# Two attention stages taken out of the scheduler's hands: every engine issues in emission order there

## The chip, the cores and the metric

The kernel runs on one core of a Trainium2 chip. The metric is the device time of one execution in microseconds. Before the change the median of 3 runs is 2639.24 us (2636.28 to 2641.58). The engines are named as in the profile: PE (TensorE matmul), PEld (its weight load), DVE (VectorE), ACT (ScalarE), POOL (GpSimd), SP (SyncE, which issues the DMAs).

## The reference

Two layers of a streaming encoder on 1024 tokens of width 1024, batch 1. Cut to what matters:

```python
for layer in range(DEPTH):                       # DEPTH = 2
    h = modulate(rms_norm(x, ln_mix_g[layer]), sh1, sc1)
    if layer % 2 == 0:
        mix = even_mixer(...)   # q,k,v,u = split(h @ w_in); concat[A, B] @ w_out
    else:
        mix = odd_mixer(...)    # cq..cg, dq,dk,dv = split(h @ w_in); concat[C, D] @ w_out
    x = x + g1[:, None, :] * mix
    x = x + g2[:, None, :] * swiglu(modulate(rms_norm(x, ...), sh2, sc2), w_in, w_out)

# A: 8 heads of 64, softmax over the own and 8 previous chunks of 64 frames, with a position bias
# B: state space model, complex diagonal scan over time, then gelu and a sigmoid gate (GLU)
# C: retention, 4 heads of 128:
scores = jnp.einsum('bhid,bhjd->bhij', qn, kn) * intra_decay
out = (jnp.einsum('bhij,bhjd->bhid', scores, vn)
       + jnp.einsum('bhid,bhde->bhie', qn * q_decay[:, :, None], state))
state = state * chunk_decay[:, None, None] + jnp.einsum('bhjd,bhje->bhde', kn * k_decay[:, :, None], vn)
# ... then (o - mu) * rsqrt(var + EPS) * norm_g, times silu(gate)
# D: stick-breaking attention, 8 heads of 64, blocks of 128 queries
log_1m_beta = jnp.where(causal, -jax.nn.softplus(z), 0.0)
between = lax.cumsum(log_1m_beta, axis=3, reverse=True) - log_1m_beta
w = jnp.where(causal, jnp.exp(jax.nn.log_sigmoid(z) + between), 0.0)
```

## The kernel before, in words

The program emits its instructions from Python generators. A generator yields where its next part has to wait, with the number of ticks to wait; `pipe.tick` advances all of them by one tick. The Tile framework then orders what was emitted: it knows which instruction needs which, and its scheduler chooses, on each engine, in which order they are issued. Only the order within an engine can change. What an instruction needs from another engine is a semaphore wait, and the PSUM banks and the numbered buffers of a pool (`bufs=`) are given out in turn, so that an instruction may also wait for the last reader of its buffer.

The first stage, AB, is `ab_phase` (61 steps). Each step starts one attention unit, `a_unit`: one head and 128 queries. It computes up to two groups of scores (L498, tile `mm` in three banks), adds the bias and takes the maximum on DVE (L597, L600), the exponential on ACT (L605), transposes on PE (L510), copies them out on ACT (L512, tile `pts`), and weighs the values on PE (L521). After four units of both heads of a pair, half a head pair is finished: a reciprocal (L617), a broadcast on POOL (L619), transposes (L626), then L630 on ACT, L631 on DVE, L632 on ACT and L633 on DVE, each needing the one before. Every five steps `s5_block` handles a block of the state space model: loads (tiles `u`, `m`, `e`), matmuls (L964), on DVE six operations (L970 to L972, twice), four scans (L976) and a complex product (L698 to L703, helper `cmul`), then matmuls again (L985, L987). Near the end, `glu` follows.

The second stage, CD, is `cd_phase`: 32 steps n of four ticks. Each step has one `c_tile` (retention, one head and 128 tokens) and one `d_unit` (stick-breaking, one head, the query blocks i and 7 - i). In `c_tile` PE projects 128 tokens in four parts of six 512-column matmuls (L248 to L250, tile `mm`); DVE makes L1078 and L1079 of it, ACT the copies L1080 and L1082, POOL the sum L1084; PE transposes that (L1089), ACT copies it (L1091), DVE scales it (L1092, L1094); PE makes the scores and the new state (L1097, L1099), DVE masks them (L1101, L1108), PE multiplies with values and state (L1112, L1114) into a bank `ob`; DVE takes mean and variance of it (L1117, L1118), POOL the power (L1119, L1120), and DVE normalises (L1122, tile `co`). Every fourth step `c_tail` adds a gate (L1132 on ACT, L1133 on POOL, L1135 on DVE, L1139 on PE, L1146 on ACT).

In `d_unit` PE makes three groups of scores (L498, tile `at`, four banks for all of CD), DVE adds the mask to two of them (L1185), ACT takes two sigmoids of each (L1188, tile `w`, and L1189, tile `b`), DVE runs two product scans over `w` (L1197; together 1152 columns), and L1199 multiplies them into `b`. Three ticks later PE transposes `b` (L510), ACT copies it (L512), and in every second step PE weighs the values (L521). Between the ticks a weight stream (`pump`) loads the next projection weights: a cast on ACT (L141) and a subtraction on POOL (L142).

Of the kernel before, what the change touches and what calls it, by code (L numbers as in the profile page):

```python
# [1368 lines left out]
def build(ctx, tc, I, out):  # L1369
    k = Trunk(ctx, tc, I, out)  # L1370
    nc, pipe = tc.nc, k.pipe
    k.cond()


    with tc.tile_pool(name="pp", bufs=1, reuse_waits="tile") as pp:
        with tc.tile_pool(name="first", bufs=1, reuse_waits="tile") as xp:
            k.first(pp, xp)
        with tc.tile_pool(name="heads", bufs=1, reuse_waits="tile") as hp:
            with tc.tile_pool(name="qk", bufs=1, reuse_waits="tile") as qp:
                right = ExitStack()  # L1380
                sp = right.enter_context(tc.tile_pool(name="set0", bufs=1, side="right", reuse_waits="tile"))
                k.stream.low = nc.vector
                for n, _ in enumerate(k.a_dense(qp)):
                    if n == 2:
                        setup = k.s5_setup(sp)
                        pipe.start(setup)
                    if n in (19, 32):
                        pipe.start(k.ada(qp, 0, 2 if n == 19 else 4))
                    if n == 38:
                        k.a_open(hp)  # L1390
                    if n == 46:
                        assert setup.gi_frame is None
                        right.close()
                        ap = right.enter_context(tc.tile_pool(name="mixa", bufs=1, side="right", reuse_waits="tile"))
                        k.pp = pp
                    pipe.tick(*([k.a_step(hp, ap, n - 46)] if n >= 46 else []))
                k.stream.low = nc.gpsimd
                pipe.tick(k.a_step(hp, ap, 2))
            k.ab_phase(hp, ap, 3)
            right.close()  # L1400
            k.pp = None
    with tc.tile_pool(name="xp0", bufs=1, reuse_waits="tile") as xp:
        x = [xp.tile([P, T], F32, name=f"x{n}") for n in range(NK)]
        for n in range(NK):
            nc.sync.dma_start(out=x[n], in_=I["x"][n])
        pipe.start(k.ada(xp, 0, 3))
        k.out_proj(xp, 0, x, [0, 1, 2, 4, 5, 6, 7, 3], 5, [(0, 4), (0, 3)], [k.ada(xp, 0, 5)])

        def done(n, h):
            if h:  # L1410
                nc.sync.dma_start(out=k.xd[n], in_=x[n])
            k.stat(xp, x[n], n, h)
            if n == NK - 1:
                pipe.start(k.norm(xp, x, h, [(1, 1), (1, 0)]))

        k.ffn(xp, 0, x, done, [lambda l=l, p=p: k.ada(xp, l, p) for l, p in ((1, 1), (1, 0), (1, 2), (1, 4), (1, 3))])
        for t in range(4):
            pipe.tick(k.v_tile(xp, "hf", k.wdv, t))
            pipe.tick()
        pipe.drain()  # L1420


    with tc.tile_pool(name="dense1", bufs=1, reuse_waits="tile") as dp:
        for n, _ in enumerate(k.d_dense(dp)):
            pipe.tick()
            if n == 1:
                for t in range(4, NT):
                    pipe.tick(k.v_tile(dp, "ve", k.wdv, t))
                    pipe.tick()
                k.wdv.free()  # L1430
    right = ExitStack()
    cp = right.enter_context(tc.tile_pool(name="mixc", bufs=1, side="right", reuse_waits="tile"))
    with tc.tile_pool(name="mixd", bufs=1, reuse_waits="tile") as dp:
        k.c_setup(cp)
        k.cd_phase(dp, cp)
    with tc.tile_pool(name="xp1", bufs=1, reuse_waits="tile") as xp:
        x = [xp.tile([P, T], F32, name=f"x{n}") for n in range(NK)]
        for kk in (0, 1, 2, 4, 5, 6):
            pipe.tick(k.mix_split(kk))
        pipe.tick(k.mix_split(3, 512))  # L1440
        for n in range(NK):
            nc.sync.dma_start(out=x[n], in_=k.xd[n])
        pipe.tick()
        while k.tail.gi_frame is not None:
            pipe.tick()
        right.close()
        k.out_proj(xp, 1, x, [0, 1, 2, 4, 5, 6, 7, 3], 1, [(1, 4), (1, 3)], [k.ada(xp, 1, 5)])

        def done(n, h):
            nc.sync.dma_start(out=out[n, :, h * 512:h * 512 + 512], in_=x[n][:, h * 512:h * 512 + 512])  # L1450

        k.ffn(xp, 1, x, done)
# [93 lines left out]
```

## Time and profile before

| | us |
|---|---|
| median of 3 runs (range) | 2639.24 (2636.28 to 2641.58) |
| the profiled execution | 2628.13 |
| its span | 2626.3 |
| busy in the span: PE, DVE, POOL, ACT | 2535.4, 1134.9, 809.5, 708.9 |
| stage AB (262 to 475 us of the span): PE, DVE, ACT, POOL busy of 213 | 190.25, 107.00, 145.29, 44.52 |
| stage CD (1448 to 1805 us): PE, DVE, ACT, POOL busy of 357 | 340.44, 242.03, 172.55, 127.79 |

The span is the profiled execution without what lies around it (1.8 us here). Busy time adds the drawn lengths of an engine's instructions, overlaps counted once. The mean granted clock of PE in the span is 0.992 of full speed. The rest of the span is dense projections and feed-forward layers, where PE is busy nearly all the time.

### The profile page before, as it was taken

The page shows a single profiled execution, that of the slowest core. Times are in us where ns is not written, and L with a number is a line of the kernel's source. Part 1 is how long each engine was busy: PE and PEld are TensorE (multiplying, and loading weights), DVE is VectorE, ACT ScalarE, POOL GpSimd, SP SyncE. Part 2 cuts the span into 40 slices and gives each one's busy share as a digit, 9 for nine tenths or more (in the row PEclk, how much of TensorE's full clock was granted, in tenths as well). Part 3 has the DMA queues.
Part 4 walks back from the last instruction along what each step waited for, and adds up shares of the span by engine and source line. Part 5 has one row for each costly group of instructions (what it writes and reads, how often), then busy time and mean ns, then how long its engine had stood idle before and what let it go on. Part 6 is the DMA issues. An engine that isn't in the chain of part 4 may idle for free. (4 is left out here: it accounts for less than half of the span.)

```text
span 2626.3 us, 32531 instructions
## 1 busy us (share of the span) xinstructions
PE 2535.4 (97%) x12912; PEld 2104.9 (80%) x12912; DVE 1134.9 (43%) x2058; ACT 708.9 (27%) x1293; POOL 809.5 (31%) x538
## 2 busy tenths in 40 slices
PE   6999898999999999999999999999999999999999
PEld 4898776777888888888788778887788888888887
DVE  6576563474333322222531566765632222222223
ACT  4332568322111111111232444544231111111100
POOL 3465003423222222232212143423243333333311
PEclk9999999999999999999999999999999999999999
DMA  7287764543233311111234333224311111111101
GB/s 282 92 248 211 211 179 154 184 145 108 93 113 112 113 49 48 48 49 49 87 109 145 87 104 102 68 76 156 112 65 49 49 50 49 50 50 49 49 9 64
DMA packets 145479, 267.12 MB, mean 102 GB/s; under 512 B 34416, under 2 KB 82224, under 8 KB 144560
## 3 DMA queue, kind: packets, MB, share of 16 engines
q1 hardware_dynamic: 145328, 265.05, 31.7%
q8 instruction: 102, 1.67, 0.3%
q14 instruction: 49, 0.40, 0.1%
HBM read 221.22 MB, written 45.88 MB: 102 GB/s over the span
## 5 line engine op out<-in xcount | busy, mean ns | idle before, releaser
L249 PE MATMUL mm<-HT,whl 128*128 128x512 f32 x1744 | 680.3, 390 | 4.5 <-DVE HT L351 4.4
L248 PE MATMUL mm<-HT,whl 128*128 128x512 f32 x1744 | 680.7, 391 | 1.8 <-ACT HT L350 1.5
L250 PE MATMUL mm<-HT,whl 128*128 128x512 f32 x1744 | 679.8, 390 | 0.0
L142 POOL TENSOR_TENSOR whl<-raw,whl 128x1024 fp32r<-128x1024 f32 x136 | 332.5, 2453 | 494.5 <-ACT whl L141 487.8
L249 PEld LDWEIGHTS mm<-HT,whl 128*128 128x128 f32 x1744 | 327.7, 188 | 76.4 <-DVE HT L351 6.7
L248 PEld LDWEIGHTS mm<-HT,whl 128*128 128x128 f32 x1744 | 327.7, 188 | 72.8 <-ACT HT L350 2.8
L250 PEld LDWEIGHTS mm<-HT,whl 128*128 128x128 f32 x1744 | 327.9, 188 | 68.5
L1342 DVE SCALAR_TENSOR_TENSOR x<-at,col,x 128x512 f32<-128x512 f32 x352 | 262.4, 750 | 268.6 <-PE at L250 268.4
L1327 DVE TENSOR_TENSOR sg<-sg,mm 128x512 f32<-128x512 f32 x88 | 60.4, 687 | 642.3 <-PE mm L250 642.3
L249 PE MATMUL at<-aT,wo 128*128 128x512 f32 x704 | 274.9, 390 | 1.9 <-POOL aT L1329 1.9
L250 PE MATMUL at<-aT,wo 128*128 128x512 f32 x704 | 274.8, 390 | 0.0
L248 PE MATMUL at<-aT,wo 128*128 128x512 f32 x704 | 273.1, 391 | 0.0
L248 PE MATMUL mm<-whl,HT 128*128 128x512 f32 (+1 forms) x688 | 249.5, 363 | 8.6 <-ACT HT L402 8.1
L249 PE MATMUL mm<-whl,HT 128*128 128x512 f32 (+1 forms) x688 | 244.8, 356 | 0.0
L142 POOL TENSOR_TENSOR wo<-raw,wo 128x1024 fp32r<-128x1024 f32 x44 | 107.4, 2464 | 442.4 <-ACT wo L141 442.4
L250 PE MATMUL mm<-whl,HT 128*128 128x512 f32 (+1 forms) x688 | 242.1, 357 | 0.0
L141 ACT CAST whl<-raw 128x1024 fp32r<-128x1024 f32 x154 | 161.3, 1054 | 172.3 <-PE mm L250 164.7
L1329 POOL TENSOR_TENSOR aT<-sg,aT 128x512 fp32r<-128x512 f32 x88 | 115.2, 1309 | 289.6 <-DVE aT L1328 281.9
L1326 ACT ACTIVATE sg<-mm 128x512 f32<-128x512 f32 x88 | 52.6, 598 | 518.7 <-PE mm L250 518.7
L141 ACT CAST wo<-raw 128x1024 fp32r<-128x1024 f32 x44 | 44.0, 1046 | 494.2 <-PE at L250 488.0
L248 PEld LDWEIGHTS mm<-whl,HT 128*128 128x128 f32 x688 | 138.0, 201 | 25.7 <-ACT HT L402 10.7
L249 PEld LDWEIGHTS at<-aT,wo 128*128 128x128 f32 x704 | 132.2, 188 | 30.8 <-POOL aT L1329 2.4
(295 smaller groups left out, 3193.0 us busy)
## 6 DMA issues: line engine op xcount, KB each, us to landing
raw<-in_ffn_w_in SPq DMA_DIRECT2D x88, 512.0 KB, 3.5
raw<-in_ada_w SPq DMA_DIRECT2D x80, 512.0 KB, 4.0
raw<-in_ffn_w_out SPq DMA_DIRECT2D x44, 512.0 KB, 3.4
ada<-in_ada SPq DMA_DIRECT2D x16, 512.0 KB, 10.2
qkd<-stk SPq DMA_DIRECT2D x32, 256.0 KB, 4.8
q<-qkd SPq DMA_DIRECT2D x64, 128.0 KB, 3.9
ks<-qkd SPq DMA_DIRECT2D x32, 256.0 KB, 4.3
qkd<-stk SPq DMA_DIRECT2D x16, 512.0 KB, 3.2
```

The source lines that it names most:

```text
L141: nc.scalar.copy(hi, u.raw[:, :u.n])
L142: self.low.tensor_sub(lo, u.raw[:, :u.n], hi.bitcast(F32))
L248: mm(out, lhs.hi, rhs.hi, start=start, stop=False)
L249: mm(out, lhs.hi, rhs.lo, start=False, stop=False)
L250: mm(out, lhs.lo, rhs.hi, start=False, stop=stop)
L1326: nc.scalar.activation(sg, gu[0], AF.Silu)
L1327: nc.vector.tensor_mul(sg, sg, gu[1])
L1329: nc.gpsimd.tensor_sub(a[m].lo[:, sl], sg, a[m].hi[:, sl].bitcast(F32))
L1342: nc.vector.scalar_tensor_tensor(xh, ps, self.col[layer, 5][:, n:n + 1], xh, M, A)
```

## The change

Both calls are wrapped in `tc.manual_schedule(engines=None)`. In it the scheduler doesn't reorder: on every engine, the queue of SP that issues the DMAs included, the instructions stand in the order in which Python emits them. Nothing is computed otherwise, and the rest of the program is scheduled as before. Line numbers above L1399 stay, those below move by one or two.

```diff
                 k.stream.low = nc.gpsimd
                 pipe.tick(k.a_step(hp, ap, 2))
-            k.ab_phase(hp, ap, 3)
+            with tc.manual_schedule(engines=None):
+                k.ab_phase(hp, ap, 3)
             right.close()
             k.pp = None
...
         k.c_setup(cp)
-        k.cd_phase(dp, cp)
+        with tc.manual_schedule(engines=None):
+            k.cd_phase(dp, cp)
```

DVE in CD, one step in the middle of a head pair, before (`at` of L1185 is a bank of scores, `w` of L1197 the long and the short scan):

```order
L1122 TENSOR_SCALAR co<-at,cmv 128x128
L1185 TENSOR_TENSOR at<-at,d_mask 128x128
L1101 TENSOR_TENSOR cat<-at,c_dm 128x128
L1108 SCALAR_TENSOR_TENSOR cst<-cst,at 128x128
L1197 SCALAR_TENSOR_TENSOR w<-one,w 128x1024
L1078 TENSOR_TENSOR ra<-mm,ccs 128x256
L1079 TENSOR_TENSOR rb<-mm,ccs 128x256
L1199 TENSOR_TENSOR b<-b,w 128x1151
L1117 BN_STATS cbs<-at 128x6
L1092 TENSOR_TENSOR qkt<-at,c_qd 128x128
L1094 TENSOR_SCALAR ckd<-cr,c_kd 128x128
L1118 BN_AGGR cmv<-cbs 128x2
```

and after:

```order
L1122 TENSOR_SCALAR co<-at,cmv 128x128
L1078 TENSOR_TENSOR ra<-mm,ccs 128x256
L1079 TENSOR_TENSOR rb<-mm,ccs 128x256
L1185 TENSOR_TENSOR at<-at,d_mask 128x128 x2
L1101 TENSOR_TENSOR cat<-at,c_dm 128x128
L1108 SCALAR_TENSOR_TENSOR cst<-cst,at 128x128
L1092 TENSOR_TENSOR qkt<-at,c_qd 128x128
L1094 TENSOR_SCALAR ckd<-cr,c_kd 128x128
L1197 SCALAR_TENSOR_TENSOR w<-one,w 128x128
L1197 SCALAR_TENSOR_TENSOR w<-one,w 128x1024
L1199 TENSOR_TENSOR b<-b,w 128x1151
L1117 BN_STATS cbs<-at 128x6
```

The masks now stand directly behind L1079 and ahead of L1092 and L1094, which stand ahead of both scans; before, the long scan came ahead of L1078 and L1079, and L1092 behind L1199.

PE in CD, the place where the third group of scores (`at_11439` before, `at_11567` after) is issued; `mm` is the projection of the same or the next step, and the groups ahead of it are `at_11436` before (21 rows ahead of the third) and `at_11558` and `at_11564` after. Before:

```order
L249 MATMUL mm_11570<-whl_10901,HT_425 128x512
L250 MATMUL mm_11570<-whl_10901,HT_425 128x512
L248 MATMUL mm_11570<-whl_10901,HT_467 128x512
L249 MATMUL mm_11570<-whl_10901,HT_467 128x512
L250 MATMUL mm_11570<-whl_10901,HT_467 128x512
L248 MATMUL mm_11570<-whl_10904,HT_509 128x512
L249 MATMUL mm_11570<-whl_10904,HT_509 128x512
L250 MATMUL mm_11570<-whl_10904,HT_509 128x512
L1097 MATMUL at_11380<-qkt_11383 128x128
L498 MATMUL at_11439<-ks_11016,q_11373 128x384 x2
```

and after:

```order
L498 MATMUL at_11558<-ks_11024,q_11483 128x384 x2
L498 MATMUL at_11564<-ks_11024,q_11483 128x384 x2
L498 MATMUL at_11567<-ks_11024,q_11483 128x384 x2
L248 MATMUL mm_11575<-whl_10780,HT_246 128x512
L249 MATMUL mm_11575<-whl_10780,HT_246 128x512
L250 MATMUL mm_11575<-whl_10780,HT_246 128x512
L248 MATMUL mm_11575<-whl_10780,HT_273 128x512
L249 MATMUL mm_11575<-whl_10780,HT_273 128x512
L250 MATMUL mm_11575<-whl_10780,HT_273 128x512
```

The projection matmuls that stood between the second group and the third now stand behind the third, which needs L1122 of the step to free its bank.

DVE in AB, around a block of the state space model (`t`, `w`, `x`) and the attention units (`pw`, `ast`, `af`), before:

```order
L597 ISA pw,ast<-mm,abias 128x320
L597 ISA ast 128x1
L972 TENSOR_TENSOR w<-t_3405,t_3406 128x256
L597 ISA pw,ast<-mm,abias 128x320
L597 ISA ast 128x1
L600 TENSOR_TENSOR ast<-ast 128x1
L976 SCALAR_TENSOR_TENSOR w<-r_76,w 128x128 x2
L698 TENSOR_TENSOR t_3405<-e,w 128x2x127
L597 ISA pw,ast<-mm,abias 128x320
L597 ISA ast 128x1
L699 TENSOR_TENSOR t_3406<-e,w 128x2x127
L600 TENSOR_TENSOR ast<-ast 128x1
```

and after, at the end of half a head pair:

```order
L600 TENSOR_TENSOR ast<-ast 128x1
L617 RECIPROCAL arc<-arc 128x8
L631 TENSOR_TENSOR af<-af,av 128x512
L633 TENSOR_TENSOR HT<-af,HT 128x512
L976 SCALAR_TENSOR_TENSOR w<-r_76,w 128x128 x4
L698 TENSOR_TENSOR t_3566<-e,w 128x2x127
L699 TENSOR_TENSOR t_3567<-e,w 128x2x127
L700 TENSOR_TENSOR x_2741<-t_3566,t_3567 128x2x127
L701 TENSOR_TENSOR t_3566<-e,w 128x2x127
L702 TENSOR_TENSOR t_3567<-e,w 128x2x127
L703 TENSOR_TENSOR x_2741<-t_3566,t_3567 128x2x127
```

The scans and the complex product now stand in one piece, with no L597 between them (the six operations L970 to L972 likewise stand together ahead of an L597), and L631 and L633 stand next to each other.

## Rows read from the trace of the kernel before

**Rows 1.** The profile's page, busy time of each engine (share of the span).
```profile
PE 2535.4 (97%) x12912; PEld 2104.9 (80%) x12912; DVE 1134.9 (43%) x2058; ACT 708.9 (27%) x1293; POOL 809.5 (31%) x538
```

**Rows 2.** Windows by stage: busy per engine (instructions), granted clock, DMA.
```profile
262.00:475.00 213.00, 190.25 (x1412) 152.02 (x1411) 107.00 (x387) 145.29 (x307) 44.52 (x35) 0.98 0.62 175
...
1448.00:1805.00 357.00, 340.44 (x2127) 282.49 (x2126) 242.03 (x445) 172.55 (x424) 127.79 (x116) 0.98 0.30 87
```

**Rows 3.** Waits of PE in 1448 to 1805: total, times, longest.
```profile
PE at L1089 <- ACT b L1189: 9.8, 7, 2.3
```

**Rows 4.** Timeline of POOL, third and last step of CD: start, duration.
```profile
1469.32 1.39 POOL L1084 TENSOR_TENSOR cr<-ra,rb 128x256 f32<-128x256 f32 x1 [14.37 <-PE at L1089]
...
1789.72 1.71 POOL L1084 TENSOR_TENSOR cr<-ra,rb 128x256 f32<-128x256 f32 x1 [2.14 <-DVE rb L1079]
```

**Rows 5.** Timeline of PE, first projection matmul of 23 and what follows.
```profile
1646.19 0.39 PE L248 MATMUL mm<-whl,HT 128*128 128x512 f32 x1
...
1651.42 0.38 PE L1097 MATMUL at<-qkt 128*128 128x128 f32 x2
```

**Rows 6.** Timeline of DVE within one step of CD.
```profile
1645.70 0.41 DVE L1079 TENSOR_TENSOR rb<-mm,ccs 128x256 f32<-128x256 f32 x1
1646.03 1.34 DVE L1199 TENSOR_TENSOR b<-b,w 128x1151 f32<-128x1151 f32 x1
1647.30 0.29 DVE L1117 BATCH_NORM_STATS2 cbs<-at 128x6 f32<-128x128 f32 x1
1647.51 0.27 DVE L1092 TENSOR_TENSOR qkt<-at,c_qd 128x128 f32<-128x128 f32 x1
...
1648.43 0.69 DVE L1197 TENSOR_TENSOR_SCAN w<-one,w 128x256 f32<-128x256 f32 x1 [0.37 <-ACT w L1188]
...
1652.87 0.28 DVE L1094 TENSOR_SCALAR ckd<-cr,c_kd 128x128 f32<-128x128 f32 x1
1653.15 2.02 DVE L1197 TENSOR_TENSOR_SCAN w<-one,w 128x896 f32<-128x896 f32 x1
1655.10 0.40 DVE L1078 TENSOR_TENSOR ra<-mm,ccs 128x256 f32<-128x256 f32 x1
```

**Rows 7.** Timeline of ACT in the same step.
```profile
1646.15 0.27 ACT L1080 COPY cg<-mm 128x128 f32<-128x128 f32 x1 [0.93 <-DVE rb L1079]
1646.38 0.55 ACT L1188 ACTIVATE w<-at 128x448 f32<-128x448 f32 x1
1646.83 0.54 ACT L1189 ACTIVATE b<-at 128x448 f32<-128x448 f32 x1
...
1653.44 1.25 ACT L512 COPY pts<-at 128x512 f32<-128x512 f32 x3
1654.54 0.43 ACT L1091 COPY qkt<-at 128x256 f32<-128x256 f32 x1
```

**Rows 8.** Timeline of DVE, normalisation in an earlier step.
```profile
1626.41 0.18 DVE L1118 BATCH_NORM_AGGREGATE cmv<-cbs 128x2 f32<-128x6 f32 x1
...
1627.61 0.41 DVE L1122 TENSOR_SCALAR co<-at,cmv 128x128 f32<-128x128 f32 x1 [0.40 <-POOL cmv L1120]
```

**Rows 9.** Groups by line, 1448 to 1805: busy, mean ns; idle before.
```profile
L1135 DVE TENSOR_TENSOR co<-co,ce 128x512 f32<-128x512 f32 x7 | 13.5, 1923 | 0.2
...
L141 ACT CAST whl<-raw 128x1024 fp32r<-128x1024 f32 x16 | 16.7, 1071 | 0.6 <-PE mm L250 0.3
```

**Rows 10.** Groups of DVE in 262 to 475; instructions of line L964.
```profile
L976 DVE TENSOR_TENSOR_SCAN w<-r,w 128x128 f32<-128x128 f32 x32 | 12.2, 423 | 0.1
...
L633 DVE TENSOR_TENSOR HT<-af,HT 128x512 fp32r<-128x512 f32 x7 | 5.0, 715 | 3.1 <-ACT HT L632 3.1
...
L964 PE MATMUL at<-u,m x128: 272/273/477, 281.2 to 386.9; 128*64 128x128 f32 x128
```

**Rows 11.** Timeline of PE at its longest wait in CD, and a window.
```profile
1466.60 2.15 PE L510 MATMUL at<-ident,b 128*128 128x128 f32 x9 [3.94 <-DVE b L1199]
...
1460.00:1470.00 10.00, 4.97 (x20) 3.80 (x20) 9.23 (x12) 6.24 (x17) 0.68 (x1) 0.67 0.25 71
```

## The prediction

> **What bounds the kernel now.** I read the page first. TensorE (PE) is busy for 2535.4 us, 97% of the span [rows 1]; over the whole program nothing else comes near it. Since the edit touches two stages only, the next view is the windows by stage [rows 2]. In the first attention stage (262 to 475 us, "AB") PE is busy 190.25 of 213 us; in the second (1448 to 1805 us, "CD") 340.44 of 357. So 22.75 and 16.56 us are all that shorter PE waits could give back by this count. It flatters PE, though, because ends of matmuls are modelled: in the timeline 23 projection matmuls start within 5.23 us [rows 5], 0.227 us each, while each is drawn 0.39 long. A stage can therefore be held up by a chain over several engines although PE looks nearly full.
>
> The list of waits names that chain for CD: what PE waits for most is the second sigmoid (L1189), 9.8 us in 7 waits [rows 3]. The rate of the stage I take from the rotary add of POOL, which runs once a step: from the third step to the last it goes from 1469.32 to 1789.72 us, 29 steps of 11.05 us [rows 4]. PE's own work in a step is less: 24 projection matmuls at 0.227 (5.4 us) and the scores, transposes and weighing, which the timeline lets me put at 3 us in a step without weighing and 5 in one with it; 8.4 and 10.4 us. These are estimates from start times.
>
> **What the change does.** No instruction is added but the order's own bookkeeping; everything stands where the Python code emits it. Three moves matter.
>
> In CD on PE, the third score group used to stand behind the projection matmuls; the 5.23 us run [rows 5] lay between the second group and the third. Now the three groups are adjacent and the third needs the bank that L1122 reads, so PE stops until VectorE (DVE) has normalised the step's output, with the next step's projection queued behind that wait. On DVE, the copy L1092, which needs ScalarE's (ACT) L1091, now stands ahead of both scans. Before, the long scan started while ACT still copied transposed weights; now it starts only after three such copies and L1091.
>
> So each step becomes one loop, and I add it up by start-to-start times of the trace where two instructions follow one another: L1122 0.41 [rows 8]; L1078 0.40 [rows 6]; from the start of L1079 to L1080 0.45 (1645.70 to 1646.15) [rows 6, 7]; L1080 and L1082, 0.23 each, 0.46; six sigmoids over 2 x 1152 columns at the 0.45 per 448 columns seen (1646.38 to 1646.83), 2.31; three copies L512, 1.10 (1653.44 to 1654.54); L1091 0.43 [rows 7]; L1092 0.27; L1094 0.28 (1652.87 to 1653.15); the long scan 1.95 (1653.15 to 1655.10); the short scan 0.69; L1199 1.27 (1646.03 to 1647.30); L1117 0.21 [rows 6]; and from L1118 through two POOL instructions to the next L1122 1.20 us (1626.41 to 1627.61) [rows 8]. The sum is 11.43 us, against 11.05 now: 0.38 x 32 = 12 us.
>
> Two things are inserted into this loop. L1135 stands between L1079 and the masks, once per four steps; its mean is 1.92 us [rows 9], so 8 x 1.92 = 15 us. Before, it lay beside waits. Of the 16 weight casts L141 half stand on ACT ahead of the sigmoids: 8 x 1.07 us [rows 9] = 9 us; the others follow L1091 and lie beside the scans. L1146 and L1132 also follow L1091: nothing, while DVE scans behind them. CD: 12 + 15 + 9 = +36 us. Bounds: if each operation in the loop costs its full duration instead of its spacing, a step is about 12.4 us and CD +67; if the loop overlaps a little more than I see and the inserted work fits in, it stays at PE's and the chain's present pace, 0. I take the sum by spacings, because neighbours in these rows do overlap so.
>
> In AB, the state-space chain on DVE loses its mixing with the attention units. Before, L597 instructions stood between its pieces; now six operations run in one piece and ten in another, about 0.42 us each [rows 10], so a unit's L597 can wait 2.5 or 4.2 us, and the three score banks stop PE behind it. The present pace is 15.0 us a block (first matmuls of the eight blocks from 281.2 to about 386, seven intervals) [rows 10], and a block begins every five ticks, so a tick, in which one unit's L597 is due, is 3.0 us. The longer piece exceeds it by 1.2. I charge half of that, since the banks hold one unit and a half: 0.6 x 8 = 5 us. Secondly the end of each half head: L631 and L633 are now in one place, with ACT's L632 between them, and DVE holds everything behind L633 until L632 is done. The row of L633 shows that wait (3.1 us in 3) and 0.72 us for the operation [rows 10]; with L631 and L632 of about the same size DVE is shut for some 2.0 us, eight times, 16 us. Thirdly, at the start, loads that were issued early now follow in emission order, and the first weighing waits for values just written: a guess of 4 us, about one tick. AB: 5 + 16 + 4 = +25. Bounds: 0, since DVE is busy only 107 of 213 us [rows 2] and may absorb the stalls, and +45, if each half head also drains the pipeline of units.
>
> **The sum.** The profiled execution took 2628.13 us: 2628 + 36 + 25 = 2689. That execution lies 0.42% below the median of the three timed runs, 2639.24, so scaled by 1.0042 the median becomes 2700 us.
>
> **Rivals.** *Faster.* Order by emission distance may flow better than the present order: if DVE's two pieces fit into its idle time, AB could give back the 22.75 us in which PE is not busy [rows 2], and CD stays at 11.05 us with its inserted work hidden. That gives 2605, or 2616 scaled. It decides as soon as AB gains more than CD's loop loses. For it speaks DVE at half load in AB; against it the CD loop, which is at 11.43 us before anything is inserted. The chance is 0.10.
>
> *No change.* Both orders might come to the same pace, with the third score group waiting as long as PE used to spend on the projection ahead of it: 2639, within 0.2% (5 us, about what a measurement of this kernel can tell). The order does move a great deal, so this would be cancellation: 0.06.
>
> *Much slower, by the clock.* [...] In my loop PE idles between 1 and 3 us a step, in two waits. If such waits brought the clock to 0.67 in every step, 8.4 and 10.4 us of PE work would become 12.5 and 15.5, a mean of 14.0, and CD would take 32 x (14.0 - 11.43) = 82 us more: 2771, scaled 2783. Chance 0.09. [...]
>
> **How the numbers follow.** The forecast, slower through both loops, has 0.75, and 2700 us is its sum. Its own range, from the bounds (0 + 15 to 67 + 45, where 15 allows that not both stages sit at their lowest), is 2654 to 2751. Of the rivals, part of the clock's case and the edge of no change are taken in: 2645 to 2770. Faster 0.10, same 0.06, slower 0.84.
>
> **What would show it.** In the changed profile CD's rotary adds should stand 12 us apart on average, PE's waits should name L498 behind L1122 and L1089 or L510 behind L1189, and DVE's should name L1091 ahead of L1092. In AB the waits for L631, L633 and L597 should have grown, and the granted clock should stay above 0.95. The prediction is wrong if the step stays near 11 us or L1135 is hidden, if AB's blocks come closer than 15 us, or if the clock drops throughout CD.

## The result, and the profile after

The changed kernel takes 2746.89 us (median of 4 runs, 2736.22 to 2752.25), the kernel before 2640.41 beside it (4 runs, 2636.28 to 2643.53). The ratio is 1.0399, with a 95% interval of 1.0363 to 1.0436: slower by 106 us, where 61 were forecast. The profiled execution took 2752.25 us, 124 more than that of before; it is the longest of its four while that of before was shorter than any of these four, so parts read from the two traces add up to more than 106.

The page of the changed kernel: span, and busy time by engine.

```profile
span 2750.4 us, 32583 instructions
...
PE 2559.9 (93%) x12912; PEld 2130.6 (77%) x12912; DVE 1118.7 (41%) x2058; ACT 701.6 (26%) x1291; POOL 771.7 (28%) x538
```

PE has the same 12912 matmuls as in [rows 1], drawn 25 us longer, in a span 124 us longer: for most of the difference it stands still, and some of its matmuls are slower. The windows by stage of the changed kernel (columns as in [rows 2]) say where:

```profile
262.00:540.00 278.00, 213.69 (x1439) 176.05 (x1438) 111.81 (x389) 141.98 (x303) 41.54 (x35) 0.82 0.48 136
...
1520.00:1905.00 385.00, 337.95 (x2111) 281.62 (x2111) 223.24 (x442) 158.85 (x416) 85.67 (x112) 0.97 0.25 71
```

In AB 64 of 278 us are without a matmul and the granted clock is 0.82; before it was 0.98 [rows 2]. In CD it is 0.97, against 0.98; this window leaves out a long wait at the start of the stage, which is shown below. Such windows have edges that I chose, so the loss is better measured between instructions that both kernels have. First the kernel before: the view of one line, with shortest, median and longest duration in ns and the first and last start in us. L597 spans AB, the loads L947 its state space blocks, L1188 CD.

```profile
L597 DVE CUSTOM_DVE_ANT_0 pw<-mm,abias x96: 258/486/692, 268.4 to 457.0; 128x320 f32<-128x320 f32 x64, 128x128 f32<-128x128 f32 x8, 128x256 f32<-128x256 f32 x8, 128x384 f32<-128x384 f32 x8
...
L947 SPq DMA_DIRECT2D e<-ed x8: 325/404/544, 277.2 to 386.4; - x8
...
L1188 ACT ACTIVATE w<-at x96: 277/492/658, 1459.5 to 1795.2; 128x512 f32<-128x512 f32 x24, 128x384 f32<-128x384 f32 x24, 128x448 f32<-128x448 f32 x16, 128x320 f32<-128x320 f32 x16
```

The same lines of the changed kernel:

```profile
L597 DVE CUSTOM_DVE_ANT_0 pw<-mm,abias x96: 283/487/692, 270.0 to 521.5; 128x320 f32<-128x320 f32 x64, 128x128 f32<-128x128 f32 x8, 128x256 f32<-128x256 f32 x8, 128x384 f32<-128x384 f32 x8
...
L947 SPq DMA_DIRECT2D e<-ed x8: 319/320/423, 275.6 to 408.8; - x8
...
L1188 ACT ACTIVATE w<-at x96: 282/534/662, 1522.8 to 1892.8; 128x512 f32<-128x512 f32 x24, 128x384 f32<-128x384 f32 x24, 128x448 f32<-128x448 f32 x16, 128x320 f32<-128x320 f32 x16
```

- AB, first to last L597: 188.6 before, 251.5 now, **+63**. Its state space blocks (first to last L947) grew from 109.2 to 133.2, +24; what follows them (the last block, the remaining attention units and the GLU; "the GLU part" below), from 70.6 to 112.7, +42.
- From the first L597 to the first L1188: 1191.1 before, 1252.8 now. The growth is AB's; between the last L597 and the first L1188 there are 1002.5 and 1001.3 us.
- CD, first to last L1188: 335.7 before, 370.0 now, **+34**.
- From the last L1188 to the end of the span: 831.1 before, 857.6 now, **+26**. Nothing was forecast here.

In CD the rotary add of POOL, which answers to [rows 4], in the timeline of the changed kernel (start, duration, and in brackets the idle time before it):

```profile
1551.81 0.74 POOL L1084 TENSOR_TENSOR cr<-ra,rb 128x256 f32<-128x256 f32 x1 [1.25 <-PE at L498]
...
1902.11 0.73 POOL L1084 TENSOR_TENSOR cr<-ra,rb 128x256 f32<-128x256 f32 x1 [1.25 <-DVE rb L1079]
```

29 steps take 350.3 us, 12.08 each, against 11.05 [rows 4]. What PE waits for in 1505 to 1905 us (total, times, longest), where [rows 3] had the second sigmoid at the top:

```profile
PE at L498 <- DVE co L1122: 25.4, 14, 2.1
PE at L498 <- DMA q<-qkd: 14.2, 1, 14.2
PE at L1089 <- ACT b L1189: 5.2, 9, 0.7
```

The second of these lines is one wait of 14.2 us, at the start of the stage. Where CD starts in the timeline of PE, first before (the projection of CD's first steps, `mm<-whl,HT`, and the first scores):

```profile
1442.30 0.39 PE L248 MATMUL mm<-whl,HT 128*128 128x512 f32 x1
...
1458.62 1.48 PE L498 MATMUL at<-ks,q 128*128 128x128 f32 x8
```

and changed (the last matmul of the dense projection ahead of CD, and the first scores):

```profile
1507.17 0.39 PE L250 MATMUL mm<-HT,whl 128*128 128x512 f32 x1
1521.75 2.56 PE L498 MATMUL at<-ks,q 128*128 128x128 f32 x6 [14.19 <-DMA q<-qkd]
```

Before, until `q` was loaded, PE ran 72 projection matmuls of CD, those of three steps; in emission order the first scores stand ahead of them, and PE waits for the load.

And in AB, 262 to 540 us, first for PE:

```profile
PE mm L498 <- DVE ast L597: 18.0, 8, 5.0
PE at L626 <- POOL af L619: 16.0, 5, 7.8
```

then for DVE:

```profile
DVE pw L597 <- PE mm L498: 54.1, 18, 7.4
DVE af L631 <- ACT af L630: 39.8, 7, 15.8
```

These two lists belong together: PE waits for DVE to empty a score bank, and DVE for PE to fill one.

### The profile page after: what moved, and what is told of

Same layout as the page of the kernel before. It is cut to its first block, busy times and chain, and to the rows that moved or that the text cites. A ratio compares the mean times of both kernels' runs of the same rounds, so it can differ in the third digit from the quotient of the medians.

```text
span 2750.4 us, 32583 instructions
## 1 busy us (share of the span) xinstructions
PE 2559.9 (93%) x12912; PEld 2130.6 (77%) x12912; DVE 1118.7 (41%) x2058; ACT 701.6 (26%) x1291; POOL 771.7 (28%) x538
## 4 chain that ended last, share of the span: by engine, by line
PE 74%; DVE 11%; DMA 5%; ACT 4%; POOL 3%; issue 2%; SPq 1%; ACTq 0%; DVEq 0%; POOLq 0%
PE mm L248 16%; PE mm L249 16%; PE mm L250 16%; PE at L249 6%; PE at L248 6%; PE at L250 6%; DVE w L1197 2%; DMA raw<-in_ada_w 2%; PE at L510 1%; PE av L521 1%; DVE b L1199 1%; POOL whl L142 1%; PE mm L498 1%; DVE HT L351 1%; DVE ada L288 1%
## 5 line engine op out<-in xcount | busy, mean ns | idle before, releaser
L248 PE MATMUL mm<-HT,whl 128*128 128x512 f32 x1744 | 681.7, 392 | 10.3 <-ACT HT L641 7.6
L249 PE MATMUL mm<-HT,whl 128*128 128x512 f32 x1744 | 680.4, 390 | 2.8 <-DVE HT L351 2.6
L142 POOL TENSOR_TENSOR whl<-raw,whl 128x1024 fp32r<-128x1024 f32 x136 | 327.9, 2419 | 564.0 <-ACT whl L141 551.7
L248 PEld LDWEIGHTS mm<-HT,whl 128*128 128x128 f32 x1744 | 328.1, 188 | 81.7 <-ACT HT L641 8.0
L249 PEld LDWEIGHTS mm<-HT,whl 128*128 128x128 f32 x1744 | 328.3, 188 | 73.9 <-DVE HT L351 4.7
L249 PE MATMUL at<-aT,wo 128*128 128x512 f32 x704 | 275.6, 391 | 1.9 <-POOL aT L1329 1.9
L248 PE MATMUL at<-aT,wo 128*128 128x512 f32 x704 | 273.1, 391 | 0.0
L248 PE MATMUL mm<-whl,HT 128*128 128x512 f32 (+1 forms) x688 | 256.2, 372 | 9.4 <-ACT HT L402 8.1
L249 PE MATMUL mm<-whl,HT 128*128 128x512 f32 (+1 forms) x688 | 246.8, 359 | 0.0
L250 PE MATMUL mm<-whl,HT 128*128 128x512 f32 (+1 forms) x688 | 244.1, 360 | 0.0
L142 POOL TENSOR_TENSOR wo<-raw,wo 128x1024 fp32r<-128x1024 f32 x44 | 106.7, 2445 | 442.0 <-ACT wo L141 421.0
L141 ACT CAST whl<-raw 128x1024 fp32r<-128x1024 f32 x154 | 160.6, 1053 | 167.2 <-PE mm L250 163.4
L141 ACT CAST wo<-raw 128x1024 fp32r<-128x1024 f32 x44 | 44.0, 1046 | 496.2 <-PE at L250 488.0
L248 PEld LDWEIGHTS mm<-whl,HT 128*128 128x128 f32 x688 | 139.3, 203 | 28.1 <-ACT HT L402 10.7
L249 PEld LDWEIGHTS at<-aT,wo 128*128 128x128 f32 x704 | 132.5, 188 | 30.9 <-POOL aT L1329 2.4
```

Of the source, the lines that this page charges most:

```text
L141: nc.scalar.copy(hi, u.raw[:, :u.n])
L142: self.low.tensor_sub(lo, u.raw[:, :u.n], hi.bitcast(F32))
L248: mm(out, lhs.hi, rhs.hi, start=start, stop=False)
L249: mm(out, lhs.hi, rhs.lo, start=False, stop=False)
L250: mm(out, lhs.lo, rhs.hi, start=False, stop=stop)
```

## The experiments

All are compared with the kernel before on the same chip, in four rounds (E1 to E4, E5 to E8, E9 to E11, E12). "Cost" is the difference of the medians.

| run | what is in emission order | median, us | ratio (95%) | cost, us |
|---|---|---|---|---|
| e1_ab_only | AB | 2695.73 | 1.0227 (1.0204 to 1.025) | 58 |
| e2_cd_only | CD | 2693.56 | 1.0227 (1.0197 to 1.0258) | 56 |
| e3_cd_steps | CD's 32 steps, not its first loads and last ticks | 2672.42 | 1.0137 (1.0116 to 1.0157) | 35 |
| e4_ab_dve | AB, DVE alone | 2669.81 | 1.0132 (1.0105 to 1.0158) | 32 |
| e5_ab_late | AB, half heads spread over ticks | 2684.58 | 1.0186 (1.0169 to 1.0203) | 48 |
| e6_ab_pe | AB, PE alone | 2655.47 | 1.0068 (1.0048 to 1.0087) | 19 |
| e7_cd_early | as E3, L1122 emitted earlier | 2661.47 | 1.0102 (1.0081 to 1.0123) | 25 |
| e8_cd_early_sched | nothing; L1122 emitted earlier | 2647.09 | 1.0041 (1.0027 to 1.0055) | 11 |
| e9_cd_free | as E7, POOL and SP left free | 2659.13 | 1.0083 (1.005 to 1.0115) | 22 |
| e10_cd_even | as E9, weighing spread over two steps | 2675.11 | 1.0145 (1.0117 to 1.0172) | 38 |
| e11_ab_first | as E1, new units ahead of old work | 2707.11 | 1.0259 (1.023 to 1.0289) | 70 |
| e12_ab_pool | as E5, two memsets on POOL | 2673.72 | 1.0159 (1.0128 to 1.019) | 45 |

**E1 and E2: each stage alone.** E1 keeps the first of the change's two `with` lines, E2 the second.

```diff
-        with tc.manual_schedule(engines=None):
-            k.cd_phase(dp, cp)
+        k.cd_phase(dp, cp)
```

> Emission order in the first stage (AB) alone, the second as before. By the trace of the changed kernel the last L597 comes 251.5 us after the first there, 188.6 before: if the stages add, this kernel is 60 to 66 us above the kernel before (about 2703). My prediction's terms for AB give 25 (2665). Rival: the two stages interact, for instance through weight loads that slip, and AB alone costs under 45.

> Emission order in the second stage (CD) alone. If the stages add: 32 steps at about 12.0 us instead of 11.05, some 30 to 35 us, and some 26 us behind the last step, where the changed kernel's PE waits for L1135 and L641; together +58 to +62 (about 2700). My prediction's term gives +36 (2676), if what comes behind the last step were an effect of AB.

58 and 56 us, each some 2 us below what was expected, make 114, against 106 for both together: within the intervals the stages add, and each costs more than its term (25 and 36).

**E3: the steps of CD without its end.** The region is put around the loop over the 32 steps; the ticks behind it, in which the last units are finished, are left to the scheduler with the output projection that follows.

```diff
-        for n in range(32):
+        with self.tc.manual_schedule(engines=None):
+            for n in range(32):
...
-        with tc.manual_schedule(engines=None):
-            k.cd_phase(dp, cp)
+        k.cd_phase(dp, cp)
```

> CD in emission order for the 32 steps, but the ticks that drain it are left to the scheduler. Theory: what is lost behind the last step is lost because the scheduler may not mix the stage's end with the output projection, so most of the 26 us come back: 15 to 26 us below the run with all of CD in emission order (2674 to 2685). Rival: the projection can't be moved up across the steps in any case, because its inputs come late; then under 8 us come back (above 2692).

Of E2's 56 us, 21 are gone. The loads of keys and values ahead of the loop are outside E3's region too, but the third L1084 starts at 1488.85 us, against 1488.37 in E2: what was gained was gained at the end. What happens there is seen on PE. The timeline of the changed kernel (start, duration, operation, idle before it):

```profile
1918.69 1.12 PE L1139 MATMUL at<-ident,co 128*128 128x128 f32 x4 [6.68 <-DVE co L1135]
1927.36 1.65 PE L248 MATMUL mm<-HT,whl 128*128 128x512 f32 x3 [7.56 <-ACT HT L641]
```

and of E3:

```profile
1839.43 1.22 PE L248 MATMUL mm<-HT,whl 128*128 128x512 f32 x2 [2.99 <-ACT HT L641]
1841.25 1.94 PE L510 MATMUL at<-ident,b 128*128 128x128 f32 x8 [0.60 <-DVE b L1199]
...
1845.34 0.50 PE L249 MATMUL mm<-HT,whl 128*128 128x512 f32 x1
```

In E3 matmuls of the projection (L248, L249, tile `HT`) already run before and between the transposes and weighings of CD's last units. In the changed kernel none can start until the last unit's chain from DVE through ACT has come through, and PE stands for 6.68 and 7.56 us. From the last L1188 to the end of the span E3 needs 836.8 us, against 831.1 before and 857.6 with the change.

The remaining 35 us are not the steps alone. From the third L1084 to the last, 29 steps take 349.2 us in E3, 28.8 more than before. The start of the stage is in them too: from the last matmul of the dense projection to the third L1084 there are 27.2 us before, 44.6 in the changed kernel, and 41.6 in E3, where PE waits 11.2 us for `q`. These add up to more than 35, for the two traces differ by 44 us. No run left the start alone to the scheduler.

**E4 and E6: one engine of AB at a time.** The scheduler keeps all engines but one.

```diff
-            with tc.manual_schedule(engines=None):
+            with tc.manual_schedule(engines={mybir.EngineType.DVE}):
                 k.ab_phase(hp, ap, 3)
```

(E6 has `PE` in place of `DVE`; CD is left to the scheduler in both.)

> AB with only DVE held to emission order, the other engines scheduled. Theory of the prediction: DVE's order (state space operations in one piece, L631 and L633 in one place) is what costs, so most of AB's loss is there: +35 to +65 over the kernel before. Rival: it is the order on PE, where the transposes L626 wait for POOL's L619 with everything behind them, and DVE's order alone costs under 20.

> AB with only PE held to emission order, the other engines scheduled around it. DVE's order alone cost 32 us. Theory: the rest, 58 - 32, is the order on PE, with everything behind the L626 that wait for POOL: +20 to +35. Rival: a free DVE mends it, since the scheduler then places L617 and L631 to suit PE: under +12. Or PE's order contains the whole loss and DVE's is the same loss seen twice: +50 to +60.

DVE's order alone costs 32 us, PE's 19, both just below what was expected of them; together 51 of E1's 58. The 7 that are left lie within the intervals, so it is not shown that the other engines' orders cost anything; they were not fixed by themselves. In E4 L947 starts from 278.9 to 401.9 and L597 until 492.4: the blocks take 123.0 us (14 more than before) and the GLU part 90.5 (20 more). In E6 (L947 from 276.4 to 392.6, L597 until 475.0) they take 116.2 and 82.4 (7 and 12 more). So both orders lose more behind the blocks than in them.

**E5: the half heads.** If DVE, shut behind L633, is the loss, then emitting the last operations of a half head some ticks later should give it back.

```diff
             return
+        yield 1
         rb = self.at_bank()
...
         nc.scalar.copy(hi, f)
+        yield 1
         nc.vector.tensor_sub(lo, f, hi.bitcast(F32))
```

> AB alone in emission order, but the end of half a head is spread over ticks: the transposes L626 are emitted one tick after the broadcast L619, and L633 one tick after L632. Theory: each of the eight half heads shuts PE and DVE for several us (blocks with such an end take 20 to 24 us in the changed trace, those without 16 to 17), so 20 to 45 us of AB's 58 come back: 2650 to 2676. Rival: the state space operations in one piece are the cost and the half heads only stand beside it; then under 8 us come back (above 2688).

10 of 58 us come back, below the lower end of the expectation. PE's waits for L619 are gone from the top of its list, where they were 16.0 us, but the wait only moves. DVE's list of E5 in 262 to 530 us:

```profile
DVE pw L597 <- PE mm L498: 64.6, 21, 12.9
```

against 54.1 in the changed kernel.

**E12: the memsets behind a load.** DVE also waits for the bias that `a_head` loads (16.8 us in 4 waits in the changed kernel, 23.4 in 5 in E5), before its two memsets there. E12 is E5 with these on POOL.

```diff
-        nc.vector.memset(bt[0:64, 576:640], NEG)
-        nc.vector.memset(bt[64:128, 0:64], NEG)
+        nc.gpsimd.memset(bt[0:64, 576:640], NEG)
+        nc.gpsimd.memset(bt[64:128, 0:64], NEG)
```

> The run with the half heads spread over ticks again (AB alone in emission order, 48 us above the kernel before), but the two memsets of the bias tile (L584, L585) are on POOL instead of DVE. In that run's trace DVE stands 23 us at L584 for the bias load, in order ahead of the next L597. Theory: these waits are part of what AB lost and come back nearly whole, because DVE's L597 stops PE: 12 to 23 us less, 2661 to 2673. Rival: while DVE stands there PE and ACT still have work, or the next L597 waits for the same load; then under 5 us come back (above 2679).

1.0159 against E5's 1.0186, with intervals that overlap: a few us at most, where 12 to 23 were expected. Again the wait is another one instead: DVE at L597 for PE's L498, 75.5 us.

**E11: new units first.** In each tick the new unit's scores and its L597 are emitted ahead of everything that is due, so that no L597 stands behind a piece of the state space chain.

```diff
+    def tick_first(self, *gens):
+        self.now += 1
+        due = [g for d, g in self.live if d <= self.now]
+        self.live = [(d, g) for d, g in self.live if d > self.now]
+        for g in gens:
+            self.start(g)
+        for g in due:
+            self.start(g)
...
-            pipe.tick(*gens)
+            (pipe.tick if n == 46 else pipe.tick_first)(*gens)
```

> AB alone in emission order, but in every tick the new unit's scores and L597 are emitted ahead of what is due, so that the state space pieces and L631 and L633 stand behind them and not ahead. Theory: L597 behind those pieces is what stops PE (L498 waits for L597 18 us, DVE idles for L631 40 us), so 20 to 40 us of AB's 58 come back: 2656 to 2676. Rival: the loss comes from PE's own order and from what the half heads and the GLU part need, and under 8 us come back or it is worse.

Nothing comes back: the cost is 70 us against E1's 58, with intervals that overlap. PE's waits in E11 (its lines are eleven higher: L509 is L498, L608 is L597):

```profile
PE mm L509 <- DVE ast L608: 28.0, 13, 6.3
...
PE mm L509 <- DMA q<-qkd: 16.2, 7, 5.2
```

Scores that stand earlier on PE wait for banks and loads that are not ready (18.0 and 2.2 us in the changed kernel), and everything stands behind them. The edit thus moved PE's order together with DVE's, and doesn't show what the place of L597 on DVE costs by itself.

**E7 and E8: L1122 out of CD's loop.** If L1122 is what closes the loop, then emitting L1112 to L1122 early, in the phase of L1097, should bring the step back to 11.05 us or lower. E7 does it in E3's region, E8 with everything scheduled.

```diff
             self.state = ns
-        yield 1
         ob = self.at_bank()
...
-        yield 1
         v.tensor_scalar(o[:, j], ob[:, :P], mv[:, 0:1], mv[:, 2:3], S, M)
+        yield 2
         if j == 3:
             self.tail = self.c_tail(pool, h, t // 4, gt, o)
...
-        yield 1
-        v.tensor_mul(of, of, e)
         yield 2
+        v.tensor_mul(of, of, e)
+        yield 1
         tp = self.at_bank()
```

> CD's 32 steps in emission order as in the run before, but L1112 to L1122 are emitted in the tick of the scores L1097, ahead of L1092 and the scans, and L1135 behind them. This takes L1117, L1118, POOL's two instructions, L1122 and L1135 out of the loop. Theory of the prediction: the loop is then 11.43 - 0.21 - 1.20 - 0.41 = 9.6 us, without the 15 us of L1135, and PE's 8.4 and 10.4 us a step become the bound: about 10.0 to 10.5 us a step, 18 to 34 us below the kernel before (2604 to 2620), or a little more where the stage's edges still cost. Rival: the loop does not go through L1122, and the step stays near 12: 2660 or more.

> The kernel before, all scheduled, with the same earlier emission of L1112 to L1122 and later L1135. Theory: the scheduler chooses the order itself, and what is emitted earlier changes it little: within 8 us of the kernel before. Rival: emission order is what it starts from, so that the loop is shorter here too: 15 us or more below.

E7 missed its expectation: its cost is only 10 us below E3's. The waits of L498 for L1122 are gone, and by the starts of L1084 plain steps now take 10.4 us without weighing and 11.6 with it, a mean of 11.0; with the inserted work and the changes of head pair, 27 steps from the third on take 11.46 each, while the kernel before has 11.05 with all of that. Part of that rest stands where a head pair changes, in the timeline of POOL in E7:

```profile
1541.52 0.74 POOL L1084 TENSOR_TENSOR cr<-ra,rb 128x256 f32<-128x256 f32 x1 [5.79 <-DMA raw<-in_cd_w_in_c]
...
1552.31 5.57 POOL L142 TENSOR_TENSOR whl<-raw,whl 128x1024 fp32r<-128x1024 f32 x2 [3.76 <-ACT whl L141]
1557.85 0.71 POOL L1084 TENSOR_TENSOR cr<-ra,rb 128x256 f32<-128x256 f32 x1
...
1566.16 0.72 POOL L1084 TENSOR_TENSOR cr<-ra,rb 128x256 f32<-128x256 f32 x1 [4.67 <-PE at L1099]
```

The L1084 of the new pair stands behind two subtractions L142, and comes 16.33 us after the one before; the next follows in 8.31. Together that is 24.6 against 22.0 for two plain steps, three times, 8 us. The other 4 us are in the four steps in which POOL makes the product of the gate (L1132 here, L1133 before) beside the scans: 11.46 us instead of 10.4. But the steps are less than half of E7's cost. In its trace 29 of them take 331.1 us, 10.7 more than before; the start, from the last matmul of the dense projection to the third L1084, takes 41.9, 14.6 more, with a wait of 11.3 us for `q`. The expectation gave the stage's edges no number. E8 shows that the early emission is no gain for the scheduler either: slower by 0.27 to 0.55%, 11 us where up to 8 were expected.

**E9 and E10: POOL free, weighing evened out.** E9 fixes the order of PE, DVE and ACT alone; E10 also lets the two halves of a weighing fall into two neighbouring steps, and gives the tile `pts` nine buffers in CD instead of six.

```diff
+        E = mybir.EngineType
+        with self.tc.manual_schedule(engines={E.PE, E.DVE, E.Activation}):
...
-        self.weigh(av[0][:, i * P:i * P + P], vt, [z[:i + 1] for z in pts], 0)
...
+        yield 4
+        self.weigh(av[0][:, i * P:i * P + P], vt, [z[:i + 1] for z in pts], 0)
```

> The run with the early L1112 to L1122 again, but POOL and SP scheduled; PE, ACT and DVE hold emission order. In that run's trace a step takes 11.0 us on average except at the four changes of the head pair, where POOL's weight subtractions L142 stand ahead of L1084 and of the power and a step takes 16.3. Theory: POOL's order costs 4 x 5 = 20 us, which come back: 2638 to 2648. Rival: the casts L141 on ACT or late weights are the cost, and less than 6 us come back.

> As the run before (POOL and SP free), and of the weighing L521 the part into the first bank is emitted four ticks later, in the step that has none. Steps with weighing are bound by PE at 11.6 us, steps without by the loop at 10.4. Theory: some 0.6 us go over to the shorter step, whose PE has about 1.4 us free: 16 x 0.6 = 10 us less than the run before, 2628 to 2638, at or just below the kernel before. Rival: the longer step isn't bound by PE's work but by its waits, and nothing is gained.

E9 is not told from E7 and lies above its expectation, and its trace shows why it says little: POOL's order came out the same, with the same 16.3 and 8.3 us at a change of pair, so a free POOL was not really tried. E10 is worse than E9 by 16 us, where 10 less were expected. Its steps are more even (10.5 to 11.8), but the two steps behind the first change of pair now take 13.4 and 12.5 us instead of 8.3 and 11.6. Evenly loaded steps may have nothing left to make up a stall with; but the mean granted clock from 1480 to 1835 us is lower too, 0.97 against 0.99 in E9, and the two causes were not told apart. Its PE waits most at L1111, which is L1112 of the other listings, for the second sigmoid:

```profile
PE at L1111 <- ACT b L1188: 17.2, 9, 3.4
```

None of the twelve is faster than the kernel before.

## Why the prediction was right in direction and short in size

**CD's loop: right, with the waits it named.** PE's top wait is L498 behind L1122, 14 times; L1089 waits for L1189. DVE's timeline of the changed kernel in one step, with weighing and with nothing inserted:

```profile
1757.59 0.18 DVE L1118 BATCH_NORM_AGGREGATE cmv<-cbs 128x2 f32<-128x6 f32 x1
...
1764.12 0.29 DVE L1092 TENSOR_TENSOR qkt<-at,c_qd 128x128 f32<-128x128 f32 x1 [1.92 <-ACT qkt L1091]
...
1764.52 2.60 DVE L1197 TENSOR_TENSOR_SCAN w<-one,w 128x384 f32<-128x384 f32 x2
1767.15 1.36 DVE L1199 TENSOR_TENSOR b<-b,w 128x1151 f32<-128x1151 f32 x1
...
1768.76 0.18 DVE L1118 BATCH_NORM_AGGREGATE cmv<-cbs 128x2 f32<-128x6 f32 x1
```

Both scans stand behind L1092, which waits 1.92 us for L1091, and from one L1118 to the next there are 11.17 us; the sum was 11.43. By the starts of L1084 plain steps without weighing take 11.2 us as well.

**CD's terms: 36 forecast, 35 measured in E3, and the agreement is luck.** In the changed kernel the 29 steps of L1084 take 29.9 us more than before, and each term of the sum came out smaller than forecast. The loop, at 11.17 us against 11.05, makes 4 us, not 12. L1135 makes some 12: the seven steps with it take 12.7 to 13.0 us where the clock did not fall (forecast 15 for eight; it has shrunk to 1.26 us, against 1.92 in [rows 9]). The three changes of head pair, with the casts L141 and what follows them, make 8: two steps there take 25.1 us instead of 22.3 (forecast 9 for the casts). The remaining 6 us had no term. They are five steps in which PE's granted clock was 0.77 to 0.90, against 0.98 to 1.00 in the other 24. PE's timeline shows it at the same place of two steps:

```profile
1759.23 0.61 PE L498 MATMUL at<-ks,q 128*128 128x384 f32 x2 [1.91 <-DVE co L1122]
...
1760.15 0.39 PE L250 MATMUL mm<-whl,HT 128*128 128x512 f32 x1
1760.38 0.39 PE L248 MATMUL mm<-whl,HT 128*128 128x512 f32 x1
```

```profile
1562.24 0.62 PE L498 MATMUL at<-ks,q 128*128 128x384 f32 x2 [1.92 <-DVE co L1122]
...
1563.35 0.63 PE L250 MATMUL mm<-whl,HT 128*128 128x512 f32 x1
1563.78 0.63 PE L248 MATMUL mm<-whl,HT 128*128 128x512 f32 x1
```

The second has the same instructions two head pairs earlier; its matmuls start 0.43 us apart instead of 0.23, and from one L1118 to the next DVE now takes 12.41 us (1560.59 to 1573.00), with a granted clock of 0.86 against 1.00 in the first (1757.59 to 1768.76). In E3 it is in part other steps that are slow. E3's 35 us, besides, hold the start of the stage, for which CD had no term.

**The edges of CD: priced at nothing.** This is the step that was left out: 21 us at the end by E3, and at the start a wait of 14.2 us, whose worth no run measured alone. I asked what the order does inside the stage, and not what the scheduler had carried over its edges.

**AB: the term that was mis-sized, 25 forecast, 58 measured.** That is above even its upper bound of 45; that the whole stayed in the range is owed to CD, which came out below its bound of 67. The stalls that I named are in the trace (L597, L631 and L633 all wait more, as forecast), but not at my prices.
- Half heads, 16 us, at 2.0 each: DVE waits at L631 and L633 for ACT 39.8 and 4.8 us in seven of them, where it was 8.1 and 3.1 before. What they cost is not the sum of these waits: with the half heads spread out L631 still waits 19.4 us, and 10 us come back (E5).
- Pieces of the state space chain ahead of L597, 5 us: the blocks' part did grow, by 24, to 19.0 us a block; but with L597 ahead of the pieces nothing came back (E11), so whether their place ahead of L597 is what costs stays open.
- The start, 4 us: the first L597 comes 1.6 us later.
- The GLU part, +42 us, had no term of its own; three of the eight half heads end in it, counted at 2 us each. One stall of this part, on POOL in the changed kernel:

```profile
490.48 4.67 POOL L142 TENSOR_TENSOR whl<-raw,whl 128x1024 fp32r<-128x1024 f32 x2 [7.27 <-PE mm L498]
495.11 4.96 POOL L1039 TENSOR_TENSOR go<-gz,gy 128x512 f32<-128x512 f32 x4
500.02 0.60 POOL L619 COPY af<-arc 128x512 f32<-128x512 f32 x1
```

and on PE:

```profile
500.67 1.11 PE L626 MATMUL at<-ident,af 128*128 128x128 f32 x4 [7.76 <-POOL af L619]
...
502.65 0.63 PE L248 MATMUL mm<-whl 128*128 128x512 f32 x1
503.08 0.63 PE L249 MATMUL mm<-whl 128*128 128x512 f32 x1
```

The broadcast L619 needs the reciprocal, which DVE did at 492.77, but stands behind two L142 and four L1039 until 500.02; PE stands behind L619, and DVE at L631 for 9.53 us. E4 and E6 put most of AB's loss on the orders of DVE and PE, each fixed by itself. They do not reduce it to one wait: where one was taken out (E5, E12), DVE's wait for PE at L597 grew. The shares of single waits stay open.

**The clock.** As the rival had it, with the clock at 0.67 in every step of CD (the granted clock in the window of [rows 11]), it didn't come: the mean there is 0.97, as forecast. But it did fall in some steps, as shown above, to 0.86 with a wait of 1.92 us, while in the other step with a wait of 1.91 us it is 1.00; what decides between the two these rows don't show. In AB, where I expected more than 0.95, it fell by more, from 0.97 to 0.80. The windows between the first and the last L597, before and changed:

```profile
268.40:457.00 188.60, 165.85 (x1277) 132.80 (x1278) 104.94 (x380) 127.36 (x284) 31.21 (x27) 0.97 0.66 184
```

```profile
270.00:521.50 251.50, 187.19 (x1291) 154.49 (x1289) 108.73 (x383) 130.42 (x286) 30.43 (x27) 0.80 0.50 141
```

Behind the wait of 7.76 us matmuls start 0.43 us apart (502.65, 503.08), nearly twice the 0.227 of [rows 5], and the granted clock from 500.67 to 503.50 us is 0.50. Of the 63 us between the two windows 42 are time without a matmul, and 21 are longer matmuls of nearly the same number. So by an estimate from these drawn lengths a third of AB's growth is the clock and two thirds are waits; no run filled PE's pauses, so it is not shown whether the clock would then have stayed up.

**The rivals.** Faster and no change are excluded by the interval. In CD an order of the same steps without the loop through L1122 comes to 11.46 us a step over all kinds of step, not below the scheduler's 11.05 (E7).

## What to carry to other kernels

A region in fixed order is also a fence: price its two edges, by asking which instructions of the neighbouring stages stood inside it before. In fixed order, count an engine's stalls at every place where its queue mixes two chains of work, the short last part included, and don't take a wait's length for its price: here E5 cut PE's 16.0 us for L619 to 2.7 and 10 us came back, and E12 took away DVE's 23.4 us at the memsets and gained a few us at most. Where steps alternate between two loads, as in E7, take the longer of loop and engine in each kind of step, not in their mean. And when a sum comes out right, compare its terms one by one: here three were too large, and hid that two edges and the clock had none.

## What was unexpected of the hardware

The rotary add L1084 on POOL takes 0.74 us in the changed kernel, where in plain steps it ran beside DVE's masks on a PSUM bank, against 1.39 and 1.71 in [rows 4]; over all 32 it is 23.6 us instead of 46.7. In both of those rows it runs beside L1199 of DVE, which has two operands in SBUF. The timeline of DVE in the kernel before, at the two places:

```profile
1468.76 1.36 DVE L1199 TENSOR_TENSOR b<-b,w 128x1151 f32<-128x1151 f32 x1
...
1789.50 1.34 DVE L1199 TENSOR_TENSOR b<-b,w 128x1151 f32<-128x1151 f32 x1
```

L1199 ends at 1470.12 and 1790.84, L1084 at 1470.71 and 1791.43, 0.59 us after it both times. Of the 32 L1084 of the kernel before, 24 start beside L1199 and end 0.58 to 0.60 us behind it; the other eight take 0.73 to 0.75 us. In the changed kernel seven of the eight L1135 on DVE, with two operands in SBUF as well, start 0.02 to 0.04 us behind an L1084: they take 1.25 or 1.26 us and the L1084 0.73 or 0.74, while the eighth L1135, with no L1084 beside it, takes 0.69. What makes one of the two longer is not shown. The shorter L1084 could give back little: in the kernel before only DVE at L1094 waited for it, 2.4 us in five waits.
